# Moving linear attention ahead of the last pair of softmax heads, and the output projection's first weight rows ahead of the third pair, in a two-layer decoder trunk

## The chip, the cores and the metric

The kernel runs on one core of one Trainium2 chip. The metric is the device time of one execution in microseconds (us). Five engines work side by side on a core, each through its own list of instructions: TensorE (PE in the profile) multiplies and transposes, VectorE (DVE) and ScalarE (ACT) do the elementwise work, GpSimd (POOL) sets masks, and SyncE (SP) issues the large transfers. An engine that needs another one's result waits on a semaphore.

## The reference

Two layers, each a half-step feed-forward block (ffn1), a mixer, and another half-step feed-forward block (ffn2). The change is in the mixer, on 256 rows of 1024 numbers:

```python
h = _modulate(_rmsnorm(x, mix_norm[l]), sh2, sc2)
proj = h @ mix_w_in[l]
a_q, a_k, a_v, b_u, c_q, c_k, c_v, c_r, c_g = jnp.split(proj, splits, axis=-1)
...
o_a = _merge_heads(_moba_attention(qa, ka, va))      # 8 heads of 64: causal softmax over the 256 rows
o_b = _conformer_conv(b_u, ...)                      # 256 channels: 31 taps, layer norm, swish
...
o_c = _gla(...)                                      # linear attention, 4 heads, chunks of 64 rows
o_c = _merge_heads(_rmsnorm(o_c, gla_out_norm[l])) * jax.nn.silu(c_r)
mixed = jnp.concatenate([o_a, o_b, o_c], axis=-1) @ mix_w_out[l]
x = x + gt2[:, None, :] * mixed
```

## The kernel before

All of it is float32 in and out. A weight piece comes from memory as `raw` (1 MB by one transfer of SP's queue, five buffers), is cast to a rounded high part `wh` on ACT (L342), and the rest `wl` is taken on DVE (L345); this pair of steps is `split`, and `wh` and `wl` have six buffers each, two for a piece. A product with split operands is three matmuls (L374 to L376 or L735 to L737 in the projections, L990 to L992 in the output projection). Rows that need no split are used as they came (`whole`, L987).

The mixer function `mix(l, done)` runs once per layer. Its program order around the change: projections for the softmax heads; then `attend(0)` to `attend(3)`, one call for each pair of heads, and between them the projections of linear attention. One call of `attend` is a chain over three engines: scores on PE (L865), masked maximum on DVE (L873, L877), exponentials on ACT (L396, four of them), reciprocal on DVE (L883), scaling on ACT (L885), transposes on PE (L888), copies on ACT (L889), products with the values on PE (L895), and the result's split on ACT and DVE (L707, L708). Linear attention is: keys and queries scaled by decays (L905, L906, L911), transposed keys (L922), the scores inside a chunk (L928) and their mask (L933), values to `cv` (L917), chunk states (L945, L951, L956), output (L960, L963), then its norm: square on ACT (L968), group mean on PE (L690), four steps on ACT (L396, L699, L396, L701) and DVE (L702, L703, L971, L973). The convolution is 62 small DVE instructions (L769), handed out in portions by `taps`, and then a norm of its own with the same lines L690 to L703.

The output projection adds four pieces of two 128-row blocks each into four accumulators `acc`. A block's number k says whose output it multiplies: 0 to 3 the softmax pairs, 4 and 5 the convolution, 6 and 7 linear attention.

```python
ORDER = (0, 2, 6, 4)
...
        for n, k0 in enumerate(ORDER):
            ...
            w = (whole if k0 >= 4 else split)(wo[:, k0:k0 + 2, :], [2, D])
```

A scheduler places the instructions of each engine at build time, by the program's order and its own estimate of when an operand is ready. What it printed is fixed: on the chip each engine takes its instructions in that order. Products into one accumulator stay in the program's order.

Of the kernel before, what the change touches and what calls it, by code (L numbers as in the profile page):

```python
# [8 lines left out]
F32 = mybir.dt.float32  # L9
# [4 lines left out]
ALU = mybir.AluOpType  # L14
# [3 lines left out]
P = 128  # L18
T = 256
D = 1024  # L20
KD = 8
# [21 lines left out]
DELAY = 2, 1  # L43
RAW, WHL = 5, 6
TAPS = (4, 2, 4, 4, 4, 4)
ORDER = (0, 2, 6, 4)

PLAN = {None: (0, 0, 0, 1), (0, 0): (22, 0, 0, 30), (0, 1): (0, 0, 0, 1), (0, 2): (19, 0, 5, 28), (1, 0): (15, 0, 5, 28),
        (1, 1): (0, 0, 0, 1), (1, 2): (4, 0, 2, 14)}
# [10 lines left out]
def trunk_kernel(ctx: ExitStack, tc: tile.TileContext, x, c, positions, ada_w, ada_b, ffn1_norm, ffn1_w_in,  # L60
# [4 lines left out]
    ACT, DVE, PE, POOL = nc.scalar, nc.vector, nc.tensor, nc.gpsimd  # L65
# [8 lines left out]
    def nm(s):  # L74
        uid[0] += 1
        return f"{s}_{uid[0]}"
# [5 lines left out]
    def unit(shape, dt=F32, s="u"):  # L82
        return u2.tile(shape, dt, tag="u2k", name=nm(s))
# [4 lines left out]
    def wide():  # L88
        return bank("mm")
# [621 lines left out]
    def mix(l, done):  # L711
        begin(l, 1)
        wi = mix_w_in[l].rearrange("(k p) f -> p k f", p=P)
        mixT = {}
        c2 = lambda ap: ap.rearrange("p a b -> p (a b)")

# [4 lines left out]
        def product_t(c0):  # L721
            return product(split(wi[:, :, c0:c0 + 256], [KD, 256]))

        def proj_n(c0, n):

            nk = 2048 // n
            pp = [wide(), wide()]
            for k0 in range(0, KD, nk):
                wh, wl = split(wi[:, k0:k0 + nk, c0:c0 + n], [nk, n])
                for k in range(nk):  # L730
                    for t in range(2):
                        a = high(k0 + k)[:, P * t:P * t + P]
                        b = low(k0 + k)[:, P * t:P * t + P]
                        first, last = k0 + k == 0, k0 + k == KD - 1
                        PE.matmul(pp[t][:, 0:n], a, wh(k, 0, n), start=first, stop=False)  # L735
                        PE.matmul(pp[t][:, 0:n], b, wh(k, 0, n), start=False, stop=False)  # L736
                        PE.matmul(pp[t][:, 0:n], a, wl(k, 0, n), start=False, stop=last)  # L737
            return pp
# [46 lines left out]
        def taps(n):  # L785
            for _ in range(n):
                next(conv, None)
# [20 lines left out]
        u, e = unit([P, 2, T], F32, "gu"), unit([P, 2, T], F32, "ge")  # L808
# [6 lines left out]
        G, eG = unit([P, 8, 64], F32, "G"), unit([P, 8, 64], F32, "eG")  # L815
# [13 lines left out]
        for w in range(2):  # L829
# [8 lines left out]
            for h in range(2):  # L838
# [3 lines left out]
                a, b = hd3(tmp[0]), hd3(tmp[1])  # L842
# [61 lines left out]
        pk = product_t(2304)  # L904
        DVE.tensor_mul(ke, pk, ke)  # L905
        DVE.tensor_mul(kt, pk, kt)  # L906
        attend(1)
        taps(TAPS[3])
        qt = unit([P, 2, T], F32, "qt")
        pq = product_t(2048)  # L910
        DVE.scalar_tensor_tensor(qt, pq, 0.125, c2(eG).rearrange("p (a b) -> p a b", a=2), op0=ALU.mult, op1=ALU.mult)  # L911
        attend(2)
        taps(TAPS[4])
        cv = unit([P, 2, 256], F32, "cv")
        pv = proj_n(2560, 256)
        for h in range(2):
            ACT.copy(cv[:, h, :], pv[h][:, 0:256])  # L917

        tk = bank()
        for t in range(2):  # L920
# [1 line left out]
                PE.transpose(tk[:, P * (2 * t + h):P * (2 * t + h) + P], ke[:, t, P * h:P * h + P], ident)  # L922
        ken = u.rearrange("p a (b c) -> p (a b) c", c=P)
        ACT.copy(ken, tk.rearrange("p (a b) -> p a b", a=4))

        acaus = [unit([P, 4, P], F32, "acaus") for _ in range(2)]
        pA = [bank(), bank()]
# [3 lines left out]
        for s in range(2):  # L931
            POOL.memset(acaus[s], 0.0)
            DVE.copy_predicated(acaus[s], gmask.bitcast(U32).unsqueeze(1).broadcast_to([P, 4, P]),  # L933
                                pA[s].rearrange("p (a b) -> p a b", a=4))
        attend(3)
        taps(TAPS[5])

        pS = [bank(), bank()]
        products = []
        for t in range(2):  # L940
            for n in (1, 0, 2):
                par, h = n % 2, n // 2
# [4 lines left out]
                                              cv[64 * par:64 * par + 64, h, 128 * t + 64 * s:128 * t + 64 * s + 64],  # L947
                                              start=True, stop=True))
        row(products)
        S = unit([P, 3, 2, 64], F32, "S")  # L950
        DVE.tensor_copy(S[:, 0], pS[0][:, 0:128].rearrange("p (a b) -> p a b", a=2))  # L951
        for n in (1, 2):
            par, h = n % 2, n // 2
            for t in range(2):
                o = 128 * h + 64 * t
                DVE.scalar_tensor_tensor(S[:, n, t, :], S[:, n - 1, t, :], eG[:, 4 * t + n, 63:64],  # L956
                                         pS[par][:, o:o + 64], op0=ALU.mult, op1=ALU.add)
# [14 lines left out]
        for t in range(2):  # L972
            DVE.scalar_tensor_tensor(oc[:, t, :], oc[:, t, :], cols[l][:, R_GN:R_GN + 1], cr[:, t, :], op0=ALU.mult,  # L973
                                     op1=ALU.mult)
            mixT[6 + t] = oc[:, t, :]
        taps(CK + 1)

        wo = mix_w_out[l].rearrange("(k p) n -> p k n", p=P)  # L980
        acc = [wide() for _ in range(4)]
        tile_of = lambda d: acc[d // 2][:, T * (d % 2):T * (d % 2) + T]

# [9 lines left out]

        for n, k0 in enumerate(ORDER):
            if n == 3:
                ada(AT_END[l, 1])
                done.last()
            w = (whole if k0 >= 4 else split)(wo[:, k0:k0 + 2, :], [2, D])
            if n < 3:
                for i in range(2):  # L1000
                    for d in range(KD):
                        add(d, k0 + i, i, w, n + i == 0, False)
            else:
                for d2 in range(0, KD, 2):
                    for i in range(2):
                        for d in (d2, d2 + 1):
                            add(d, k0 + i, i, w, False, i == 1)
                    for d in (d2, d2 + 1):
                        residual(tile_of(d), l, 1, d)
                        done(d)  # L1010
# [223 lines left out]
```

## Time and profile before

| what | value |
|---|---|
| median of three runs | 1053.15 us (1052.93 to 1054.54) |
| the profiled execution | 1054.32 us, of which its span 1052.6 us |
| TensorE, share of the span busy | 99% |
| VectorE, ScalarE | 81%, 57% |
| TensorE's mean granted clock | 0.996 of full speed |

The span goes from the first to the last instruction. A matmul's record overlaps the next one's, so a gap shows as idle time only when the engine really ran dry. The profile puts the idle time in brackets behind the instruction that ended it, with what released it.

### The profile page before, as it was taken

To read this page: it belongs to the slowest core of one execution; us is meant where nothing else is said; L and a number is where in the kernel's file an instruction comes from. 1 tells how busy PE (TensorE), PEld (TensorE's weight loads), DVE (VectorE), ACT (ScalarE), POOL (GpSimd) and SP (SyncE) were. 2 spreads that over 40 slices of the span, in tenths; PEclk is the share of its full clock that TensorE was granted. 3 is DMA by queue.
4 is the path that set the end of the run, shared out by engine and by line. 5 is a ranking of instruction groups with operands and counts; after the bars stand their busy time and mean duration, and the time that the engine had idled before them with its cause. 6 is when DMAs were issued, how large, how long until landed. Compare 5 with 4: busy or idle time off the path is not lost.

```text
span 1052.6 us, 17525 instructions
## 1 busy us (share of the span) xinstructions
PE 1037.0 (99%) x6892; PEld 913.1 (87%) x6892; DVE 848.8 (81%) x1408; ACT 599.2 (57%) x1061; POOL 23.0 (2%) x60
## 2 busy tenths in 40 slices
PE   8999999999999999999999999999999999999998
PEld 7899998888888988888889888888879889888887
DVE  3699878879996899998669998866899779866552
ACT  4565454458667665564457555554767666555441
POOL 6000000001000000000000000000000000000000
PEclk9999999999999999999999999999999999999999
DMA  9999989885344679999766999867343445865430
GB/s 315 369 331 349 363 294 329 303 285 170 125 143 144 229 236 322 359 326 316 235 206 220 332 328 309 287 205 239 122 158 121 160 162 190 287 202 181 157 124 21
DMA packets 177603, 251.42 MB, mean 239 GB/s; under 512 B 7514, under 2 KB 156470, under 8 KB 170352
## 3 DMA queue, kind: packets, MB, share of 16 engines
q1 hardware_dynamic: 176480, 249.97, 70.6%
q8 instruction: 54, 0.88, 0.4%
q0 software_dynamic: 1024, 0.32, 0.2%
q14 instruction: 29, 0.24, 0.1%
q10 hardware_dynamic: 16, 0.00, 0.0%
HBM read 249.23 MB, written 1.05 MB: 238 GB/s over the span
## 4 chain that ended last, share of the span: by engine, by line
PE 90%; ACT 3%; DVE 3%; DMA 2%; POOL 1%; issue 0%; POOLq 0%; DVEq 0%; ACTq 0%
PE mm L380 36%; PE mm L381 18%; PE mm L374 7%; PE mm L376 7%; PE mm L375 7%; PE mm L987 3%; PE mm L737 2%; PE mm L735 2%; PE mm L736 2%; ACT wh L342 1%; PE tp L234 1%; DMA adaraw<-in_ada_w_dram 1%; DMA pos<-in_positions_dram 1%; DVE wl L345 1%; PE tp L262 1%; DVE ab L769 1%
## 5 line engine op out<-in xcount | busy, mean ns | idle before, releaser
L345 DVE TENSOR_TENSOR wl<-raw,wh 128x1024 fp32r<-128x1024 f32 (+1 forms) x344 | 384.2, 1128 | 113.8 <-ACT wh L342 107.6
L342 ACT CAST wh<-raw 128x1024 fp32r<-128x1024 f32 (+1 forms) x344 | 332.5, 974 | 235.5 <-PE mm L380 106.2
L380 PE MATMUL mm<-hT,wh 128*128 128x512 f32 x912 | 322.7, 397 | 0.0
L381 PE MATMUL mm<-hT,wl 128*128 128x256 f32 x912 | 256.3, 282 | 0.0
L380 PE MATMUL mm<-g,wh 128*128 128x512 f32 x704 | 249.3, 398 | 0.0
L380 PEld LDWEIGHTS mm<-hT,wh 128*128 128x128 f32 x912 | 172.4, 189 | 43.0 <-DVE g L708 1.7
L381 PE MATMUL mm<-g,wl 128*128 128x256 f32 x704 | 197.6, 281 | 0.0
L374 PE MATMUL mm<-hT,wh 128*128 128x256 f32 (+1 forms) x656 | 188.1, 287 | 2.1 <-ACT wh L342 2.0
L375 PE MATMUL mm<-hT,wh 128*128 128x256 f32 (+1 forms) x656 | 186.9, 285 | 0.0
L376 PE MATMUL mm<-hT,wl 128*128 128x256 f32 (+1 forms) x656 | 186.5, 284 | 0.3 <-DVE wl L345 0.2
L381 PEld LDWEIGHTS mm<-hT,wl 128*128 128x128 f32 x912 | 171.7, 188 | 0.2
L380 PEld LDWEIGHTS mm<-g,wh 128*128 128x128 f32 x704 | 132.2, 188 | 35.0 <-ACT wh L342 2.5
L381 PEld LDWEIGHTS mm<-g,wl 128*128 128x128 f32 x704 | 133.0, 189 | 0.0
L374 PEld LDWEIGHTS mm<-hT,wh 128*128 128x128 f32 x656 | 124.9, 190 | 5.2 <-ACT wh L342 2.6
L376 PEld LDWEIGHTS mm<-hT,wl 128*128 128x128 f32 x656 | 124.8, 190 | 0.9 <-DVE wl L345 0.8
L375 PEld LDWEIGHTS mm<-hT,wh 128*128 128x128 f32 x656 | 124.5, 190 | 1.0 <-DVE hT L461 0.2
L243 DVE SCALAR_TENSOR_TENSOR adaacc<-adaraw,cact,adaacc 128x2048 f32<-128x2048 f32 (+1 forms) x59 | 123.5, 2093 | 2.1 <-DMA adaraw<-in_ada_w_dram 2.1
L553 ACT COPY ab<-mm 128x256 f32<-128x256 f32 x114 | 41.7, 370 | 53.5 <-PE mm L381 53.4
L559 DVE SCALAR_TENSOR_TENSOR xT<-mm,gate,xT 128x256 f32<-128x256 f32 x80 | 34.6, 478 | 22.7 <-PE mm L381 15.3
L554 DVE TENSOR_TENSOR ab<-ab,mm 128x256 f32<-128x256 f32 x114 | 46.3, 416 | 6.2 <-ACT ab L553 6.0
L769 DVE SCALAR_TENSOR_TENSOR ab<-hpad,cw,ab 128x256 f32<-128x256 f32 x120 | 51.0, 476 | 0.0
L737 PE MATMUL mm<-wl,hT 128*128 128x512 f32 (+1 forms) x128 | 47.6, 372 | 0.0
(231 smaller groups left out, 1062.5 us busy)
## 6 DMA issues: line engine op xcount, KB each, us to landing
raw<-in_ffn_w_in_dram SPq DMA_DIRECT2D x85, 1024.0 KB, 6.4
adaraw<-in_ada_w_dram SPq DMA_DIRECT2D x72, 1024.0 KB, 7.0
raw<-in_ffn_w_out_dram SPq DMA_DIRECT2D x32, 1024.0 KB, 6.1
raw<-in_mix_w_in_dram SPq DMA_DIRECT2D x24, 1024.0 KB, 5.6
raw<-in_ffn_w_out_dram SPq DMA_DIRECT2D x16, 768.0 KB, 5.7
raw<-in_mix_w_out_dram SPq DMA_DIRECT2D x8, 1024.0 KB, 5.0
held<-in_ffn_w_in_dram SPq DMA_DIRECT2D x12, 256.0 KB, 10.5
xn<-in_x_dram SPq DMA_DIRECT2D x2, 512.0 KB, 4.3
```

The lines of the kernel that those rows point to most:

```text
L243: DVE.scalar_tensor_tensor(part, w, cact[:, k, 0:1], part, op0=ALU.mult, op1=ALU.add)
L342: ins = ACT.copy(hs[-1][:, b:c], raw(a + b, a + c)).ins
L345: DVE.tensor_sub(ls[-1][:, b:c], raw(a + b, a + c), f32(hs[-1][:, b:c]))
L374: PE.matmul(o, wh, high, start=first, stop=False)
L375: PE.matmul(o, wh, low, start=False, stop=False)
L376: PE.matmul(o, wl, high, start=False, stop=last)
L380: PE.matmul(halves(o), wh, pair, start=first, stop=False)
L381: PE.matmul(o[:, 0:T], wl, pair[:, 0, :], start=False, stop=last)
L553: ACT.copy(t[:, s, :], o[s][:, T:2 * T])
L554: DVE.tensor_add(t[:, s, :], t[:, s, :], o[s][:, 0:T])
L737: PE.matmul(pp[t][:, 0:n], a, wl(k, 0, n), start=False, stop=last)
L769: DVE.scalar_tensor_tensor(y[:, t, :], hpad[:, t, k:k + T], w, y[:, t, :], op0=ALU.mult, op1=ALU.add)
```

## The change

Linear attention up to its norm stands ahead of `attend(3)`: the key transposes ahead of `attend(1)`, the chunk scores and their mask ahead of `attend(2)`, states, output and norm between `attend(2)` and `attend(3)`. The split of the value projection's weights (`wv`) and that of the output projection's first piece (`w0`, rows of the softmax pairs 0 and 1) stand ahead of `attend(2)`. `ORDER` takes linear attention's rows second. The states `S` are kept in a tile that is free by then.

```diff
-ORDER = (0, 2, 6, 4)
+ORDER = (0, 6, 2, 4)
...
-        attend(1)
-        taps(TAPS[3])
-        qt = unit([P, 2, T], F32, "qt")
-        pq = product_t(2048)
-        DVE.scalar_tensor_tensor(qt, pq, 0.125, c2(eG).rearrange("p (a b) -> p a b", a=2), op0=ALU.mult, op1=ALU.mult)
-        attend(2)
-        taps(TAPS[4])
-        cv = unit([P, 2, 256], F32, "cv")
-        pv = proj_n(2560, 256)
-        for h in range(2):
-            ACT.copy(cv[:, h, :], pv[h][:, 0:256])
 
         tk = bank()
...
         ACT.copy(ken, tk.rearrange("p (a b) -> p a b", a=4))
+        attend(1)
+        taps(TAPS[3])
+        qt = unit([P, 2, T], F32, "qt")
+        pq = product_t(2048)
+        DVE.scalar_tensor_tensor(qt, pq, 0.125, c2(eG).rearrange("p (a b) -> p a b", a=2), op0=ALU.mult, op1=ALU.mult)
...
-        attend(3)
-        taps(TAPS[5])
+        wv = split(wi[:, :, 2560:2816], [KD, 256])
+
+        w0 = split(wo[:, ORDER[0]:ORDER[0] + 2, :], [2, D])
+        attend(2)
+        taps(TAPS[4])
+        cv = unit([P, 2, 256], F32, "cv")
+        pv = proj_n(2560, 256, wv)
+        for h in range(2):
+            ACT.copy(cv[:, h, :], pv[h][:, 0:256])
...
-        S = unit([P, 3, 2, 64], F32, "S")
+
+        S = c2(e)[:, 0:384].rearrange("p (n a b) -> p n a b", n=3, a=2)
...
             mixT[6 + t] = oc[:, t, :]
+        attend(3)
+        taps(TAPS[5])
         taps(CK + 1)
...
-            w = (whole if k0 >= 4 else split)(wo[:, k0:k0 + 2, :], [2, D])
+            w = (whole if k0 >= 4 else split)(wo[:, k0:k0 + 2, :], [2, D]) if n else w0
```

From `attend` on, the changed kernel's line numbers are one higher (L888 is L889 there), the output projection's four higher (L990 is L994).

The first place is PE's list in the second layer, from the last pair's scores (`tp<-qkT`) to the first transposes of its softmax (`tp<-ident,tmp`). Before:

```order
L865 MATMUL tp_8822<-qkT_8140,qkT_8138 128x128
L865 MATMUL tp_8821<-qkT_8140,qkT_8138 128x128
L992 MATMUL mm_8976<-mix_8487,wl_8983 128x256
L990 MATMUL mm_8976<-mix_8487,wh_8982 128x256
...
L990 MATMUL mm_8978<-mix_8606,wh_8986 128x256
L888 MATMUL tp_8841<-ident_70,tmp_8133 128x128 [waits Activation_49]
L991 MATMUL mm_8978<-mix_8606,wh_8986 128x256
L992 MATMUL mm_8978<-mix_8606,wl_8987 128x256
L888 MATMUL tp_8841<-ident_70,tmp_8133 128x128 [waits Activation_49]
```

And in the changed kernel:

```order
L690 MATMUL tp_8872<-ge_8118,grpb_86 128x256
L866 MATMUL tp_8888<-qkT_8138,qkT_8136 128x128 [waits PE_49]
...
L994 MATMUL mm_8987<-mix_8611,wh_8715 128x256
L995 MATMUL mm_8987<-mix_8611,wh_8715 128x256
L996 MATMUL mm_8987<-mix_8611,wl_8716 128x256
L889 MATMUL tp_8907<-ident_70,tmp_8132 128x128 [waits PE_49,Activation_49]
L889 MATMUL tp_8907<-ident_70,tmp_8132 128x128 [waits Activation_49]
L889 MATMUL tp_8907<-ident_70,tmp_8132 128x128
L991 MATMUL mm_8984<-G_8125,raw_9036 128x256 [waits DMAHW1_49,DVE_49]
L991 MATMUL mm_8984<-G_8125,raw_9036 128x256
L889 MATMUL tp_8924<-ident_70,tmp_8133 128x128 [waits PE_49,Activation_49]
```

Before, 36 products of the output projection stand between the scores and the first transpose (34 in the first layer). Now it is the last three of the first piece (eight in the first layer); the products of the linear-attention rows (`mm<-G,raw`) stand behind the transposes, and the 48 products of the pairs 2 and 3 behind those.

The second place is ACT's list in the second layer at the same point: `tmp` and `nb` belong to the last pair's softmax, `rstd` to linear attention's norm, `wh` to ffn2's weights. Before:

```order
L396 ACTIVATE tmp_8133,rsum_8834<-tmp_8133,nb_8832,rq_1313_8143 128x128 [waits DVE_49]
L396 ACTIVATE tmp_8133,rsum_8834<-tmp_8133,nb_8832,rq_1313_8143 128x256
L342 CAST wh_9197<-raw_9195 128x512 [waits DMAHW5_49,PE_49]
L342 CAST wh_9197<-raw_9195 128x512
L885 ACTIVATE tmp_8133<-tmp_8133,rin_8837 128x128 [waits DVE_49]
```

And in the changed kernel:

```order
L396 ACTIVATE rstd_8875<-tp_8872,epsc_80 128x512 [waits PE_49]
L699 ACTIVATE rstd_8876<-tp_8872,hepsc_82 128x512
L396 ACTIVATE rstd_8875<-rstd_8875 128x512 [waits Activation_49]
L342 CAST wh_9201<-raw_9193 128x512 [waits PE_49]
L701 ACTIVATE rstd_8877<-rstd_8875 128x512 [waits Activation_49]
L396 ACTIVATE tmp_8132,rsum_8900<-tmp_8132,nb_8898,rq_1312_8142 128x128 [waits DVE_49]
L396 ACTIVATE tmp_8132,rsum_8900<-tmp_8132,nb_8898,rq_1312_8142 128x256
L342 CAST wh_9201<-raw_9193 128x512
L886 ACTIVATE tmp_8132<-tmp_8132,rin_8903 128x128 [waits DVE_49]
```

The four steps of the norm now stand ahead of the last pair's exponentials. In the first layer they do too, there without a cast among them and with all four exponentials ahead of the first scaling.

The third place is DVE's list in the second layer between the second pair's second reciprocal and the third pair's first maximum (`mx`). Before:

```order
L883 RECIPROCAL rin_8592<-rsum_8589 128x2 [waits Activation_49]
L769 SCALAR_TENSOR_TENSOR ab_7993<-hpad_105,cw_21_118,ab_7993 128x256 [waits DVE_49] x11
L911 SCALAR_TENSOR_TENSOR qt_8617<-mm_8628,eG_8127 128x512 [waits PE_49]
L708 TENSOR_TENSOR mix_8606<-tp_8601,mix_8606 128x256 [waits Activation_49]
L873 ISA tmp_8133,mx_8686<-tp_8678,amask_90 128x128 [waits PE_49]
```

And in the changed kernel:

```order
L884 RECIPROCAL rin_8597<-rsum_8594 128x2 [waits Activation_49]
L770 SCALAR_TENSOR_TENSOR ab_7992<-hpad_105,cw_21_118,ab_7992 128x256 [waits DVE_49] x10
L919 SCALAR_TENSOR_TENSOR qt_8622<-mm_8633,eG_8126 128x512 [waits PE_49]
L708 TENSOR_TENSOR mix_8611<-tp_8606,mix_8611 128x256 [waits Activation_49]
L770 SCALAR_TENSOR_TENSOR ab_7992<-hpad_105,cw_21_118,ab_7992 128x256 [waits DVE_49] x4
L928 COPY_PREDICATED acaus_8684<-gmask_98,tp_8686 128x512 [waits PE_49,Pool_49]
L928 COPY_PREDICATED acaus_8683<-gmask_98,tp_8685 128x512 [waits PE_49]
L770 SCALAR_TENSOR_TENSOR ab_7992<-hpad_105,cw_21_118,ab_7992 128x256 [waits DVE_49]
L874 ISA tmp_8132,mx_8727<-tp_8719,amask_90 128x128 [waits PE_49]
```

Five taps and the two masks have come in ahead of the third pair's maximum, for one tap fewer earlier.

## Rows read from the trace of the kernel before

**Rows 1.** The page: the chain that ended last, and one group (busy us, mean ns).

```profile
PE 90%; ACT 3%; DVE 3%; DMA 2%; POOL 1%; issue 0%; POOLq 0%; DVEq 0%; ACTq 0%
...
L342 ACT CAST wh<-raw 128x1024 fp32r<-128x1024 f32 (+1 forms) x344 | 332.5, 974 | 235.5 <-PE mm L380 106.2
```

**Rows 2.** Windows: length, busy PE, PEld, DVE, ACT, POOL; then granted clock.

```profile
728.00:861.50 133.50, 130.23 (x906) 112.44 (x906) 113.28 (x261) 89.33 (x182) 0.99 (x2) 0.99 0.45 150
312.00:324.00 12.00, 10.90 (x103) 10.13 (x103) 11.07 (x32) 9.65 (x25) 0.00 (x0) 1.00 0.89 285
818.78:822.20 3.42, 3.42 (x20) 2.40 (x22) 3.42 (x4) 1.94 (x5) 0.00 (x0) 0.50 0.01 4
```

**Rows 3.** Timeline of PE, second layer, third pair: start, us, what, [idle before].

```profile
815.81 0.28 PE L991 MATMUL mm<-mix,wh 128*128 128x256 f32 x1
816.40 1.53 PE L888 MATMUL tp<-ident,tmp 128*128 128x128 f32 x6 [0.31 <-ACT tmp L885]
818.74 1.55 PE L895 MATMUL tp<-tmp,va 128*64 128x256 f32 x8 [0.81 <-ACT tmp L889]
...
823.45 0.38 PE L992 MATMUL mm<-mix,wl 128*128 128x256 f32 x1
```

**Rows 4.** The same work in the first layer.

```profile
310.65 0.87 PE L895 MATMUL tp<-tmp,va 128*64 128x256 f32 x8
311.46 0.66 PE L922 MATMUL tp<-ident,ge 128*128 128x128 f32 x4
...
313.04 0.94 PE L865 MATMUL tp<-qkT,qkT 64*128 64x128 f32 x12
313.91 0.38 PE L992 MATMUL mm<-mix,wl 128*128 128x256 f32 x1
```

**Rows 5.** Timeline of PE, first layer, last pair's first transpose.

```profile
317.84 0.28 PE L990 MATMUL mm<-mix,wh 128*128 128x256 f32 x1
317.96 0.28 PE L991 MATMUL mm<-mix,wh 128*128 128x256 f32 x1
319.34 0.33 PE L888 MATMUL tp<-ident,tmp 128*128 128x128 f32 x1 [1.10 <-ACT tmp L885]
319.43 0.36 PE L992 MATMUL mm<-mix,wl 128*128 128x256 f32 x1
```

**Rows 6.** Timeline of PE, both layers: the first product of linear attention's rows.

```profile
334.49 1.78 PE L987 MATMUL mm<-G,raw 128*128 128x256 f32 x7 [0.26 <-DVE G L973]
...
843.87 1.35 PE L987 MATMUL mm<-G,raw 128*128 128x256 f32 x5 [1.61 <-DVE G L973]
```

**Rows 7.** Timeline of all engines, second layer: the third pair's softmax.

```profile
811.52 0.94 PE L865 MATMUL tp<-qkT,qkT 64*128 64x128 f32 x12
...
812.87 0.28 DVE L873 CUSTOM_DVE_ANT_0 tmp<-tp,amask 128x128 f32<-128x128 f32 x1
...
813.82 0.49 ACT L396 ACTIVATE tmp<-tmp,nb,rq 128x128 f32<-128x128 f32 x1 [1.40 <-DVE nb L877]
...
815.96 1.48 ACT L885 ACTIVATE tmp<-tmp,rin 128x128 f32<-128x128 f32 x4
```

**Rows 8.** Timeline of ACT, first layer: linear attention's norm, and what follows.

```profile
329.28 0.70 ACT L396 ACTIVATE rstd<-tp,epsc 128x512 f32<-128x512 f32 x1
...
331.65 0.62 ACT L773 ACTIVATE ab<-ab 128x512 f32<-128x512 f32 x1
```

**Rows 9.** Timeline of ACT, second layer: after the third pair's value products.

```profile
820.33 0.37 ACT L707 CAST mix<-tp 128x256 fp32r<-128x256 f32 x1 [1.12 <-PE tp L895]
820.60 0.65 ACT L917 COPY cv<-mm 128x256 f32<-128x256 f32 x2
```

**Rows 10.** Timeline of DVE, second layer, ahead of the third pair's maximum.

```profile
807.59 4.42 DVE L769 SCALAR_TENSOR_TENSOR ab<-hpad,cw,ab 128x256 f32<-128x256 f32 x11
811.93 0.68 DVE L911 SCALAR_TENSOR_TENSOR qt<-mm,eG 128x512 f32<-128x512 f32 x1
...
822.97 1.35 DVE L933 COPY_PREDICATED acaus<-gmask,tp 128x512 f32<-128x512 uint32 x2 [0.56 <-PE tp L928]
```

More of the change, by code (lines that the diff above doesn't have):

```diff
@@ L713, in mix @@
         wi = mix_w_in[l].rearrange("(k p) f -> p k f", p=P)
+        wo = mix_w_out[l].rearrange("(k p) n -> p k n", p=P)
         mixT = {}
@@ L722, in product_t, with proj_n @@
             return product(split(wi[:, :, c0:c0 + 256], [KD, 256]))
-        def proj_n(c0, n):
+        def proj_n(c0, n, w=None):
             nk = 2048 // n
@@ L728, in proj_n @@
             for k0 in range(0, KD, nk):
-                wh, wl = split(wi[:, k0:k0 + nk, c0:c0 + n], [nk, n])
+                wh, wl = w or split(wi[:, k0:k0 + nk, c0:c0 + n], [nk, n])
                 for k in range(nk):
@@ L975, in mix @@
             mixT[6 + t] = oc[:, t, :]
+        attend(3)
+        taps(TAPS[5])
         taps(CK + 1)
-        wo = mix_w_out[l].rearrange("(k p) n -> p k n", p=P)
         acc = [wide() for _ in range(4)]
```

## The prediction

> **What bounds the kernel now.** I read the chain that ended last first: 90% of the span is TensorE's [rows 1]. The kernel gets shorter only where TensorE waits or its clock is low. So I went through TensorE's timeline in both mixers for instructions with idle time in brackets, and read the windows for the clock: the whole second mixer shows 0.99, with one stretch of 3.42 us at 0.50 in it [rows 2], which is 1.2 of 2.4 GHz. The reader is to see five places. In the second layer the six transposes of the third pair wait for ScalarE, and the value products behind them again [rows 3]: from 816.09 (end of the last product) to 818.74 it is 2.65 us for six transposes, which at 0.16 us each (four of the same size take 0.66 [rows 4]) are 1.0 us of work, so 1.65 us of waiting. Right behind that the clock stands at 0.50: value products, key transposes, chunk scores and the last pair's scores take 4.71 us [rows 3], and in the first layer at full clock 3.26 [rows 4], so 1.45 us more. In the first layer the last pair's first transpose waits 1.10 us [rows 5], and the clock stays at 1.00 there [rows 2]. And in both layers the first product of linear attention's rows waits for the norm, 0.26 and 1.61 us [rows 6].
>
> **What the change takes away.** All five, if it does what it does to the order: the norm is finished long before its products in the place where they waited, the third pair's transposes have 33 products ahead of them in place of 29, and the key transposes and chunk scores stand elsewhere. That is 1.10 + 0.26 in the first layer, 1.65 + 1.45 + 1.61 in the second: 6.1 us. More isn't to be had at these places, and less if one of the waits stays; I take all of it.
>
> **What it puts in their place.** The work on every engine is the same in sum: no matmul, cast or transfer is added, and the states take one tile less. What counts is what stands between an instruction and its operand.
>
> First, the last pair's transposes. Between its scores and the first transpose there were 36 and 34 products; now there are three in the second layer and eight in the first. The 24 products of pair 2 can't come forward, since they add to accumulators that linear attention's rows must add to first, and those wait for the norm; the 24 of the last pair need this softmax itself. So TensorE waits for a whole softmax with nothing to do. The third pair shows its length: scores from 811.52, done 0.87 later (313.04 to 313.91 [rows 4]) at 812.39, first transpose at 816.40 [rows 3, 7], so 4.0 us. Against it stand products of 0.12 us each [rows 5]: three give 0.36, eight give 0.96. That is the lower bound, 3.65 and 3.05, 6.7 us together. But ScalarE now has the norm's four steps first, 2.37 us from 329.28 to 331.65 [rows 8]; it can begin them when the group mean is done, when TensorE begins the scores. In the first layer then come four exponentials, 2.14 us from 813.82 to 815.96, and 0.44 from the first scaling to the transpose [rows 3, 7]: 4.95, less scores 0.87 and eight products 0.96, so 3.1 us. In the second layer two exponentials (1.07) and two half casts, about 0.5 each (a whole one takes 0.97 [rows 1]): 4.9, less 0.87 and 0.36, so 3.65. I take 6.8 us; VectorE's steps of the norm, which stand between those of the softmax, may add 0.5 in each layer, so the upper bound is 7.8.
>
> Second, `cv`. The chunk states need the two copies to `cv`, which ScalarE makes behind the split of the third pair's result; from the end of the value products to the end of the copies it is 0.92 us, 820.33 to 821.25 [rows 9]. This was hidden, since transposes, chunk scores and the last pair's scores came next on TensorE. Now one product of 0.12 stands there in the second layer (0.8 us of waiting), and one matmul of another kind in the first, for which I take 0.4: 1.2 us. Nothing else can stand in, so 0.8 is the least.
>
> Third, the third pair's own transposes. VectorE now reaches its maximum later: ten taps at 0.40 (4.42 for eleven [rows 10]), queries and result split 0.94 (811.93 to 812.87 [rows 7, 10]), four taps 1.6, two masks 1.35 [rows 10], a tap 0.4, in all 8.3 us. They began at 807.59 [rows 10]; a split of 1.1 us ahead of them has gone elsewhere and a tap of 0.4 has come, so they begin at 806.9 and the maximum starts at 815.2, the first transpose 3.53 us later (812.87 to 816.40 [rows 3, 7]), at 818.7. TensorE had begun the third pair's scores at 811.52 [rows 7]; before that point it now does four transposes more (0.6) and eight products less (0.96), so 811.15, then nine products (1.1), chunk scores and scores (1.85, from 313.91 less 311.46 less 0.6 [rows 4]) and 33 products (3.95), which ends at 818.05. It waits 0.65 us, and some 0.4 more for the second head. Both sides are sums over many rows, and an error of 1 us is easy: the bounds are 0 and 2 us in each layer, and I take 1.2 each, 2.4 us.
>
> Fourth, small ones with one answer: in the second layer linear attention's products, among the last pair's transposes, may wait for the norm's steps on VectorE (0 to 1 us, I take 0.5), and ffn2's opening may find its operands later, because a transfer for the modulation now waits for a buffer that those products hold and VectorE's use of it stands ahead of the first residual (0 to 1, I take 0.3). The earlier split of `w0` costs nothing: VectorE does the same two subtractions, and TensorE has products of the projections to do meanwhile; without that cover it would cost their 2.3 us (1.13 each).
>
> Fifth, the clock. In the second layer some 1.65 us of waiting in 2.65 came before the fall, and the fall cost 1.45; 1.10 us in the first layer brought none [rows 2, 3, 5]. The new waits are 3.1 and 3.65 us, longer than the one that brought the fall, so I count two falls. Part of each slow stretch will lie in further waits, where it costs nothing: 1.2 us each, 2.4 together, with 0 and 2.9 as bounds. The Trainium skill says, in TensorE: Matmul & The Clock Gate, section HAM oscillation — how this bites in real kernels, that a wait for operands between groups of products re-throttles the engine, so that the next group starts cold, and it prices the loss at half of the throttled time. By that price, an estimate, two stretches of 3.42 us would cost 3.4 us in place of 2.4 and the sum would be 1.0 us higher; the row's own 1.45 is less than half of 3.42, because not all that ran in it ran on the array all the time, and I keep to it.
>
> **Sum.** New: 6.8 + 1.2 + 2.4 + 0.8 + 2.4 = 13.6 us; gone: 6.1; so 7.5 us longer. The profiled execution took 1054.32 us; its sum would be 1061.8. The median of the runs is 1.17 us lower than it, 1053.15, so I predict 1060.7 for the median. A measurement of this kernel can tell about 0.2%, 2.1 us, from no change.
>
> **Rivals.** *The cover holds (faster).* TensorE finds work behind each waiting transpose, or the softmax is done when it gets there; only `cv` is left: 1.2 less 6.1, 4.9 us shorter, 1048.3. It speaks for it that 24 products, those of pair 2, have their operands before the last pair's softmax ends. Against it: in the first layer TensorE sat 1.10 us at a transpose, and the product behind it started 0.09 us after it [rows 5], although its operands came from pairs long done: it doesn't pass a waiting instruction. It decides for faster only if all new waits but `cv` and the clock's share stay under 2.8 us together, against 6.7 that the third pair's own softmax gives for the first alone. The Trainium skill says the same in TensorE: Matmul & The Clock Gate, Part 2: What happens when you issue a matmul: weight loads may be pulled ahead, the matmuls themselves stay in program order. The trace agrees, by the 1.10 us. Chance 0.05.
>
> *Only the last pair and `cv` (no change).* The third pair's transposes find their operands ready and the clock doesn't fall: 6.8 + 1.2 less 6.1, 1.9 us longer, 1055.1. For it: my count for the third pair is near zero within its error; the clock held through 1.10 us. Against: the waits are three times that. Chance 0.12.
>
> *Everything at its upper end (slower still).* 7.8 + 1.2 + 4 + 2 + 2.9 less 6.1, 11.8 us longer, 1065. For it: DVE and ACT take norm and softmax in turns, so each late step makes the other late. Chance 0.13.
>
> **How the numbers follow.** The forecast has 0.70, and with its small terms off by one or two it spans 1057 to 1063. The range from 1055.5 to 1065 leaves out the faster case, most of the no-change case and what lies beyond the upper end. Slower by over 0.2% is the forecast and the upper case, 0.83; within 0.2% is the third, 0.12; faster 0.05.
>
> **What would show it.** In the profile after: the last pair's transposes with 3 to 4 us of idle time in front of them in each layer, released by the scaling on ScalarE, and the norm's four steps ahead of the exponentials; the chunk states with about half a us or more, released by the copies to `cv`; two stretches at clock 0.5 behind the long waits; no idle time in front of linear attention's products at their old size in the second layer, and the stretch at 818.78 at full clock. I am wrong if TensorE's idle time at the last pair's transposes is under 2 us in a layer, or if products of pair 2 run there.

## The result: 10.5 us slower

The changed kernel takes 1064.57 us (median of 5 runs, 1063.33 to 1065.29) where the kernel before, run beside it, takes 1054.03; the ratio is 1.0099, 95% interval 1.0088 to 1.011. The profiled span went from 1052.6 to 1063.6 us.

The changed kernel's page, the chain that ended last; in [rows 1] TensorE has 90% of it:

```profile
PE 87%; DVE 5%; ACT 4%; DMA 3%; issue 1%; SPq 0%; ACTq 0%
```

To see where the time went I cut out each mixer, from the first pair's first score to the next stage's first product. Windows of the kernel before (start and end, length, busy PE, PEld, DVE, ACT, POOL, granted clock):

```profile
282.66:348.22 65.56, 64.20 (x525) 55.58 (x525) 54.51 (x152) 45.58 (x106) 0.00 (x0) 1.00 0.49 161
791.91:857.60 65.69, 62.81 (x506) 55.71 (x505) 53.34 (x141) 44.75 (x104) 0.00 (x0) 0.97 0.43 144
```

The same windows of the changed kernel, and its stretches of low clock:

```profile
282.91:354.58 71.67, 68.54 (x525) 57.37 (x525) 54.77 (x151) 45.20 (x104) 0.00 (x0) 0.98 0.44 146
798.31:868.11 69.80, 64.52 (x505) 56.25 (x505) 53.32 (x139) 43.90 (x100) 0.00 (x0) 0.95 0.42 138
329.90:333.32 3.42, 3.42 (x10) 2.60 (x10) 1.58 (x4) 2.07 (x5) 0.00 (x0) 0.50 0.00 0
841.90:848.73 6.83, 6.10 (x17) 4.15 (x19) 1.11 (x4) 2.17 (x6) 0.00 (x0) 0.50 0.49 154
```

The first mixer is 6.11 us longer and the second 4.11, together 10.2 of the 11.0 us. Length less busy PE is idle time: 1.36 became 3.13 in the first mixer, 2.88 became 5.28 in the second, so 4.2 us. The other 6 us lie in a *busy* TensorE with the same instructions, 4.34 us of them in the first mixer. So idle time alone explains less than half.

The rows that answer to [rows 3, 5, 6], TensorE's timeline of the changed kernel in both mixers:

```profile
324.21 0.94 PE L866 MATMUL tp<-qkT,qkT 64*128 64x128 f32 x12
...
329.42 0.33 PE L889 MATMUL tp<-ident,tmp 128*128 128x128 f32 x1 [3.12 <-ACT tmp L886]
329.70 1.06 PE L991 MATMUL mm<-G,raw 128*128 128x256 f32 x2
...
825.03 0.33 PE L889 MATMUL tp<-ident,tmp 128*128 128x128 f32 x1 [0.48 <-ACT tmp L886]
...
829.13 0.84 PE L947 MATMUL tp<-cv,gu 64*64 64x64 f32 x24 [0.43 <-ACT cv L938]
...
836.01 0.94 PE L866 MATMUL tp<-qkT,qkT 64*128 64x128 f32 x12
...
840.86 0.83 PE L889 MATMUL tp<-ident,tmp 128*128 128x128 f32 x3 [3.36 <-ACT tmp L886]
842.63 2.07 PE L991 MATMUL mm<-G,raw 128*128 128x256 f32 x4 [0.94 <-DVE G L976]
```

The last pair's transposes wait 3.12 and 3.36 us, with a fall of the clock behind each. ScalarE's timeline in the second mixer shows what they wait for:

```profile
836.12 0.69 ACT L396 ACTIVATE rstd<-tp,epsc 128x512 f32<-128x512 f32 x1 [0.76 <-PE tp L690]
...
838.30 0.64 ACT L701 ACTIVATE rstd<-rstd 128x512 f32<-128x512 f32 x1
838.83 0.48 ACT L396 ACTIVATE tmp<-tmp,nb,rq 128x128 f32<-128x128 f32 x1
...
839.89 0.60 ACT L342 CAST wh<-raw 128x512 fp32r<-128x512 f32 x1
840.40 0.80 ACT L886 ACTIVATE tmp<-tmp,rin 128x128 f32<-128x128 f32 x2
...
843.08 0.80 ACT L886 ACTIVATE tmp<-tmp,rin 128x128 f32<-128x128 f32 x2 [0.28 <-DVE rin L884]
```

The norm's steps, with a half cast among them, fill 836.12 to 838.94; only then come the softmax's exponentials.

### The profile page after: what moved, and what is told of

Its sections match the earlier page's. It is cut to its first block, busy times and chain, and to the rows that moved or that the text cites. A ratio compares the mean times of both kernels' runs of the same rounds, so it can differ in the third digit from the quotient of the medians.

```text
span 1063.6 us, 17530 instructions
## 1 busy us (share of the span) xinstructions
PE 1043.7 (98%) x6892; PEld 915.6 (86%) x6892; DVE 849.1 (80%) x1408; ACT 599.2 (56%) x1061; POOL 22.9 (2%) x60
## 4 chain that ended last, share of the span: by engine, by line
PE 87%; DVE 5%; ACT 4%; DMA 3%; issue 1%; SPq 0%; ACTq 0%
PE mm L380 36%; PE mm L381 18%; PE mm L374 7%; PE mm L376 7%; PE mm L375 6%; PE mm L991 2%; DMA adaraw<-in_ada_w_dram 2%; DVE wl L345 2%; DMA held<-in_ffn_w_in_dram 1%; PE mm L738 1%; DVE ab L770 1%; PE mm L737 1%; PE mm L736 1%; ACT wh L342 1%; PE tp L262 1%; PE tp L234 1%
## 5 line engine op out<-in xcount | busy, mean ns | idle before, releaser
L737 PE MATMUL mm<-wh,hT 128*128 128x512 f32 (+1 forms) x128 | 47.6, 372 | 0.0
L736 PE MATMUL mm<-wh,hT 128*128 128x512 f32 (+1 forms) x128 | 47.5, 371 | 0.0
```

## The experiments

Lengths are those of the two mixers in the profiled execution, cut as above; the last column is idle PE in them (length less busy PE). Each ratio is against the kernel before as it was run beside that version (medians 1054.03 to 1054.29).

| kernel | median, us | ratio to before | mixer 1 | mixer 2 | idle 1, 2 |
|---|---|---|---|---|---|
| before | 1054.03 | | 65.56 | 65.69 | 1.36, 2.88 |
| changed | 1064.57 | 1.0099 (1.0088 to 1.011) | 71.67 | 69.80 | 3.13, 5.28 |
| e1_order_back | 1062.85 | 1.0083 (1.0069 to 1.0097) | 71.22 | 68.47 | 2.08, 4.41 |
| e2_early_split | 1059.58 | 1.0052 (1.0039 to 1.0065) | 67.51 | 68.44 | 2.62, 5.04 |
| e3_filled_wait | 1058.96 | 1.0047 (1.0034 to 1.0059) | 69.99 | 65.76 | 1.21, 2.53 |
| e4_early_gla | 1061.71 | 1.0065 (1.0051 to 1.0079) | 68.22 | 69.93 | 1.55, 4.70 |
| e5_norm_behind | 1057.87 | 1.0037 (1.0024 to 1.005) | 67.94 | 66.95 | 1.16, 3.24 |
| e6_e1_norm_behind | 1056.20 | 1.0019 (1.001 to 1.0028) | 68.82 | 64.09 | 0.93, 1.83 |
| e7_order_alone | 1068.56 | 1.0143 (1.0129 to 1.0157) | 70.96 | 74.79 | 6.38, 8.86 |
| e8_filled_before | 1054.01 | 1.0 (0.9992 to 1.0009) | 65.47 | 65.82 | 1.27, 3.45 |
| e9_second_layer_only | 1052.71 | 0.9986 (0.9977 to 0.9995) | 65.39 | 64.11 | 1.17, 1.84 |
| e10_scores_cut | 1056.15 | 1.002 (1.0011 to 1.0029) | 67.57 | 65.81 | 0.59, 1.97 |
| e11_scores_whole | 1054.89 | 1.001 (1.0001 to 1.0019) | 66.09 | 64.94 | 0.41, 2.41 |

**e1, the old order of rows in the changed kernel.**

```diff
-ORDER = (0, 6, 2, 4)
+ORDER = (0, 2, 6, 4)
```

> The changed kernel with one line put back: the output projection adds the rows of pairs 0 and 1 first, then those of pairs 2 and 3's first half as before, linear attention's third (0, 2, 6, 4). Linear attention stays ahead of the last pair and the early splits stay. TensorE's order now has 30 products (first layer) and 25 (second) between the last pair's scores and its first transpose, where the changed kernel has 8 and 3. Theory 'no cover': the cost of the change is that nothing can run during the last pair's softmax, and the clock falls behind that wait. From the scores' end to the first transpose the changed kernel takes 4.35 us and 3.98 us; 30 and 25 products of 0.12 us are 3.7 and 3.1, so 0.6 and 0.9 us of waiting stay of 3.12 and 3.36, the 0.94 us in front of linear attention's first product goes, and with them both falls of the clock, some 4 us: about 1054.7 us, between 1053 and 1057. Rival 'early norm': the norm's steps ahead of the softmax on ScalarE and VectorE make everything behind them late, whatever TensorE has to do: within 3 us of the changed kernel, 1061.5 or more.

1062.85: the theory "no cover" falls in that form (cover: products that TensorE can run while a chain on other engines isn't done). The rival's 1061.5 or more is met; e5 and e6 below take up the norm's place. TensorE's timeline of e1, second mixer, and the second head's transposes in the kernel before:

```profile
835.34 0.94 PE L866 MATMUL tp<-qkT,qkT 64*128 64x128 f32 x12
...
840.19 0.84 PE L889 MATMUL tp<-ident,tmp 128*128 128x128 f32 x3 [0.73 <-ACT tmp L886]
843.43 1.09 PE L889 MATMUL tp<-ident,tmp 128*128 128x128 f32 x3 [2.40 <-ACT tmp L886]
845.08 1.55 PE L896 MATMUL tp<-tmp,va 128*64 128x256 f32 x8 [0.57 <-ACT tmp L890]
```

```profile
831.09 0.33 PE L888 MATMUL tp<-ident,tmp 128*128 128x128 f32 x1
```

The first head's wait is what I expected (0.73 for 0.9). I had not counted the second head, which comes 3.24 us behind the first, and the clock falls within its wait (0.50 from 842.31 on, for 6.83 us). From scores to the second head's transposes it is 8.1 us. In the kernel before it is no shorter: 8.4, from 822.69 to 831.09. But there 60 products of 0.12 us lie within it. They are the 72 products of pairs 0 to 2 less four that had run before and eight that run later; in e1 47 of the 72 had run before the last pair's scores, in the stages where the change put linear attention.

**e2, the early splits alone, in the kernel before.**

```diff
+        wv = split(wi[:, :, 2560:2816], [KD, 256])
+        w0 = split(wo[:, ORDER[0]:ORDER[0] + 2, :], [2, D])
         attend(2)
...
-        pv = proj_n(2560, 256)
+        pv = proj_n(2560, 256, wv)
```

> The kernel before with the early splits alone: the split of the value weights and of the output projection's first rows ahead of the third pair's call, linear attention and the order of rows as before. TensorE then has 33 products ahead of the third pair's first transposes in place of 29, and more behind them. Theory 'the early split costs nothing and takes the third pair's wait away': the second layer's 1.65 us and the 1.45 us of low clock behind it go: about 1051 us, between 1049.5 and 1052.5. Rival 'the early split brings the loss': its casts and subtractions stand in the way of the softmax's steps, so the transposes wait as long as before or longer: 1054 or more, and if it were the whole cause of the loss, 1064.

1059.58: the rival's side, but not by its mechanism. TensorE's timeline of e2, second mixer: the third pair's first transpose, the last pair's, the norm's matmuls and the first product of linear attention's rows:

```profile
818.54 0.27 PE L889 MATMUL tp<-ident,tmp 128*128 128x128 f32 x1
...
828.77 0.33 PE L889 MATMUL tp<-ident,tmp 128*128 128x128 f32 x1 [0.36 <-ACT tmp L886]
...
839.61 1.09 PE L690 MATMUL tp<-ge,grpb 128*128 128x256 f32 x4
...
847.32 1.22 PE L989 MATMUL mm<-G,raw 128*128 128x256 f32 x2 [3.10 <-DVE G L976]
```

The third pair's wait is gone, as the first theory said, and the clock stays up there; the last pair waits 0.36 us. But 21 products of pairs 0 and 1 now run ahead of the last pair in the second mixer, where 4 did, so only 6 are left between the norm's matmuls and linear attention's products, which wait 3.10 us, with a fall of the clock at 846.90. In the first mixer 14 are left and the wait is 2.62 us, there without a fall. The cover was spent early and is missing at the end.

**e3, the wait of the changed kernel filled.**

```diff
+                for _ in range(fill if s == 0 else 0):
+                    PE.transpose(pT[:, 0:P], ident, ident)
...
-        attend(3)
+        attend(3, 18)
```

> The changed kernel with 18 transposes of the identity (18 x some 0.16 us = 2.9 us) put on TensorE between the last pair's scores and its first transposes in each mixer, written to a place that the true transpose writes over. They use the time of the wait and add nothing to the result. Theory 'the clock pays a part': the waits of 3.12 and 3.36 us become work of the same length, so the time of the waits stays, but the clock doesn't fall behind them: by the rows of the changed kernel the products in the slow stretches take some 1.4 us (first layer) and 2.5 us (second) more than at full clock, so about 1061 us, between 1059.5 and 1062.5. Rival 'the wait alone': the low clock costs nothing, because what runs in it would wait for linear attention's norm anyway: within 0.8 us of the changed kernel, 1063.8 to 1065.4.

1058.96, 5.6 us faster than the changed kernel although 36 instructions were added. Windows of e3, and its timeline:

```profile
282.00:351.99 69.99, 68.78 (x543) 58.17 (x543) 54.77 (x151) 45.20 (x104) 0.00 (x0) 1.00 0.45 150
795.84:861.60 65.76, 63.23 (x524) 56.48 (x523) 53.47 (x139) 43.70 (x101) 0.00 (x0) 1.00 0.43 142
```

```profile
324.17 2.19 PE L889 MATMUL tp<-ident 128*128 128x128 f32 x18
326.11 0.36 PE L997 MATMUL mm<-mix,wh 128*128 128x256 f32 x1
...
328.51 0.33 PE L891 MATMUL tp<-ident,tmp 128*128 128x128 f32 x1 [1.21 <-ACT tmp L886]
...
838.55 0.33 PE L891 MATMUL tp<-ident,tmp 128*128 128x128 f32 x1 [1.61 <-ACT tmp L886]
```

The clock reads 1.00 in both. The filling takes 1.94 us (324.17 to 326.11) in each mixer; busy PE without it is 66.84 and 61.29 us, against 68.54 and 64.52 in the changed kernel. So the low clock cost 1.70 and 3.23 us in the changed kernel's profiled execution, and in the second mixer idle time fell by 0.8 besides: there the scheduler has also put some of linear attention's products elsewhere among the transposes, and their wait of 0.94 us is gone. In the first mixer the order is otherwise the same. The theory holds in its direction, with a larger price than it named: 1058.96 lies below its 1059.5.

**e4, linear attention early, alone** (no early splits, old order of rows).

```diff
-        w0 = split(wo[:, ORDER[0]:ORDER[0] + 2, :], [2, D])
...
-            w = (whole if k0 >= 4 else split)(wo[:, k0:k0 + 2, :], [2, D]) if n else w0
+            w = (whole if k0 >= 4 else split)(wo[:, k0:k0 + 2, :], [2, D])
```

> Linear attention up to its norm ahead of the last pair, alone: the order of the rows as before (0, 2, 6, 4) and no early split. TensorE has 34 and 29 products between the last pair's scores and its first transpose, but only some 16 and 18 between the third pair's scores and its transposes, where the changed kernel has 34 and 33. Theory 'no cover': the wait goes to the third pair: by the changed kernel's rows its transposes are ready 4.7 us behind the scores' end in the second layer, 18 products are 2.2, so 2.4 us of waiting and a fall of the clock there, up to 2 us in the first layer, against e1's about 1054.7: about 1058 us, between 1055.5 and 1061. Rival 'early norm': the loss belongs to the place of linear attention itself and comes back whole: 1062 or more.

1061.71, between the two. The third pair's wait in the second mixer is 2.30 us, as expected, with its fall of the clock; but the last pair waits again as well, 1.62 and 0.57 us, and brings another fall.

**e5 and e6, the norm behind the last pair.** The edit is the same on e4 and on e1:

```diff
+        attend(3)
+        taps(TAPS[5])
         oc, osq = G.rearrange("p (a c) b -> p a (c b)", a=2), e
...
-        attend(3)
-        taps(TAPS[5])
         taps(CK + 1)
```

> e4_early_gla (linear attention early, rows in the old order, no early split) with the last pair's call put between linear attention's output and its norm, so that ScalarE and VectorE come to the last pair's softmax first and to the norm's steps behind it. Theory 'two chains at once': norm and softmax together take the 7 to 9 us from the scores to the second head's transposes, and 24 to 34 products of 0.12 us don't last that long. With the norm behind, the last pair's waits (1.62 and 0.57 us in the second layer, 0.82 and 0.59 in the first) and the fall of the clock there go, some 5 us, and up to 1 us comes back in front of linear attention's products: about 1057 us against 1061.7, between 1055 and 1059. The third pair's wait of 2.3 us stays. Rival 'the cover is spent': products used up before the last pair are missing whatever stands first, so the wait goes over to the norm whole: 1060 or more.

> The same step from e1_order_back (which has the early splits): the last pair's call between linear attention's output and its norm. Theory 'two chains at once': e1's waits at the last pair (0.50, 0.87 and 0.57 us in the first layer, 0.73, 2.40 and 0.57 in the second) and its falls of the clock (some 1.4 and 3.2 us) go, 10 us, and 1 to 3 us come back in front of linear attention's products, which have 24 products ahead of them where e2_early_split had 14 and 6 and waited 2.62 and 3.10: about 1056 us, between 1053.5 and 1058.5, and by the third pair's wait better than e5_norm_behind. Rival 'the cover is spent': 1060 or more, the wait standing in front of linear attention's products with a fall of the clock behind it.

1057.87 and 1056.20, 3.8 and 6.7 us faster than e4 and e1, where 4.7 and 7 were expected, so the rival falls. ScalarE's timeline of e6, second mixer:

```profile
833.48 0.49 ACT L396 ACTIVATE tmp<-tmp,nb,rq 128x128 f32<-128x128 f32 x1
...
835.61 1.48 ACT L886 ACTIVATE tmp<-tmp,rin 128x128 f32<-128x128 f32 x4
...
840.40 0.69 ACT L396 ACTIVATE rstd<-tp,epsc 128x512 f32<-128x512 f32 x1 [0.29 <-PE tp L690]
```

Softmax first, then the norm. TensorE's timeline of e6:

```profile
836.05 0.33 PE L889 MATMUL tp<-ident,tmp 128*128 128x128 f32 x1
...
838.43 0.87 PE L896 MATMUL tp<-tmp,va 128*64 128x256 f32 x8 [0.84 <-ACT tmp L890]
...
845.60 1.78 PE L991 MATMUL mm<-G,raw 128*128 128x256 f32 x7 [0.22 <-DVE G L978]
```

Both heads' transposes find their operands, linear attention's products wait 0.22 us where they waited 1.61 [rows 6], and the clock doesn't fall in either mixer. The second mixer is 1.6 us *shorter* than in the kernel before; the first stays 3.3 us longer, with less idle time than before: its TensorE is busy for 67.89 us in place of 64.20, at full clock.

Two things moved with this edit. From the end of the last pair's scores to the second head's transposes it is 5.2 us in e6 (831.65 to 836.80) where e1 took 7.2 (836.21 to 843.43): the chain is shorter with the norm behind it. And the scores come earlier in TensorE's order: 26 of the 72 products have run before them, not 47, so 45 lie in that stretch, not 25. The times fit "two chains at once"; how much of the gain each of the two brings was not separated.

**e7, the order of rows alone, in the kernel before.**

```diff
-ORDER = (0, 2, 6, 4)
+ORDER = (0, 6, 2, 4)
```

> The kernel before with the changed order of rows alone (0, 6, 2, 4): linear attention's rows come ahead of pair 2's, everything else in its old place. Theory 'no cover': in the kernel before 24 and 17 products stand between the norm's first matmul and linear attention's products, which wait 0.26 and 1.61 us; without them the waits are about 3.3 and 3.7 us, so 5.1 us more, and each lets the clock fall, 1.5 us in each layer: about 1062 us, between 1059 and 1064.5. Rival 'the order is a detail': the 24 products of pair 2 run a little later and nothing else changes: 1054 to 1055.5.

1068.56, the slowest of all. The theory is right in sign, but 6.5 us too low and outside its range, and the loss is not where it put it. Linear attention's products wait 1.65 and 2.09 us, less than the 3.3 and 3.7 expected; here in the second mixer:

```profile
850.73 8.60 PE L987 MATMUL mm<-G,raw 128*128 128x256 f32 x32 [2.09 <-DVE G L973]
```

Besides them both heads of the last pair, the value products and both norms' matmuls wait, and the second mixer's clock falls twice (10.2 us at 0.50).

**e8, the third pair's wait of the kernel before filled** (second mixer), by the loop of e3.

```diff
-        attend(2)
+        attend(2, 10 if l == 1 else 0)
```

> The kernel before with ten transposes of the identity (10 x 0.11 us) ahead of the third pair's transposes in the second mixer alone, where it waits 0.31 and 0.81 us and the clock falls; they are written over and add nothing to the result. Theory 'the clock pays a part': the wait is 1.65 us with what drains and restarts, the transposes stand in for most of it, the clock stays up and the 1.45 us behind it go: about 1052.7 us, between 1051.8 and 1053.4. Rival 'filling costs what it takes': the same as before or up to 1.1 us more, 1054 to 1055.3.

1054.01, no change: the rival's number, though not its reason. TensorE's timeline of e8:

```profile
811.83 0.94 PE L865 MATMUL tp<-qkT,qkT 64*128 64x128 f32 x12
...
821.62 1.12 PE L865 MATMUL tp<-qkT,qkT 64*128 64x128 f32 x12
...
828.23 0.33 PE L890 MATMUL tp<-ident,tmp 128*128 128x128 f32 x1 [0.99 <-ACT tmp L885]
```

The clock stays at 1.00 and the last pair's scores come 9.79 us behind the third pair's, where they came 11.17 behind (811.52 [rows 7] to 822.69): 1.4 us gained. Then the last pair's transposes wait 0.99 us, where they had no wait, and start as late as before: 35.97 us behind the mixer's start, against 35.96. The chain there doesn't follow TensorE: VectorE comes to the maximum 0.5 us earlier, and ScalarE's cast ahead of the first scaling then waits 0.57 us for a transfer. So the 1.45 us of low clock in the kernel before, which I had booked as a gain, was paid out of a wait for the softmax behind it.

The other executions of the kernel before say the same. Their mean granted clock goes from 0.996 to 1.0, so the fall isn't in all of them, and the 19 at 0.999 or 1.0 take 1054.1 us in the mean, the nine at 0.996 1054.3.

**e9, the second mixer of e6, the first of the kernel before.**

```diff
+        early = l == 1
...
+        if early:
+            ken = key_transposes()
         attend(1)
...
-        pO = output()
+        if early:
+            pO = output()
+        else:
+            ken = key_transposes()
+            acaus = chunk_scores()
         attend(3)
         taps(TAPS[5])
+        if not early:
+            pO = output()
```

> The first mixer in the order of the kernel before, the second in that of e6_e1_norm_behind (linear attention up to its output ahead of the last pair, the early splits, the last pair's call between output and norm, old order of rows). From the last pair's first stage to the next stage e6's second mixer took 64.1 us where the kernel before took 65.7, and its first mixer 68.8 where before took 65.6. Theory 'the layers add up': 1.6 us faster than the kernel before, about 1052.7 us, between 1051.8 and 1053.6. Rival 'only moved': what the second mixer gives comes back in the stage behind it, or hung on the first mixer's order: 1054 or more.

1052.71, ratio 0.9986: the layers add up, and this version is faster than both kernels, by 1.5 us (1054.19 beside it) and 11.9 us.

**e10 and e11, what a cut in a row of scores costs.** In the changed kernel's first mixer two rows of scores are cut, each by four products, and the modulation's sums stand elsewhere. TensorE's timeline of the changed kernel, and the sums in the kernel before:

```profile
293.08 0.49 PE L866 MATMUL tp<-qkT,qkT 64*128 64x128 f32 x2
293.50 0.38 PE L375 MATMUL mm<-hT,wh 128*128 128x256 f32 x1
...
294.17 0.93 PE L866 MATMUL tp<-qkT,qkT 64*128 64x128 f32 x10
...
314.68 1.44 PE L262 MATMUL tp<-adaacc,ones 128*32 128x512 f32 x5
316.05 0.87 PE L896 MATMUL tp<-tmp,va 128*64 128x256 f32 x8
316.85 1.05 PE L262 MATMUL tp<-adaacc,ones 128*32 128x512 f32 x2
```

```profile
309.67 1.06 PE L262 MATMUL tp<-adaacc,ones 128*32 128x512 f32 x6
```

The group of the modulation's sums in the first mixer (busy us, mean ns), in the kernel before and then in the changed one:

```profile
L262 PE MATMUL tp<-adaacc,ones 128*32 128x512 f32 x8 | 2.1, 605 | 0.0
```

```profile
L262 PE MATMUL tp<-adaacc,ones 128*32 128x512 f32 x8 | 2.9, 598 | 0.0
```

e10 cuts all eight rows of the kernel before with one transpose each; e11 has the same transposes ahead of the rows. In both mixers TensorE's order differs in nothing else. The edit of e10:

```diff
+                    if len(products) == 1:
+                        products.append(PE.transpose(ss[0][:, 0:P], ident, ident))
```

> The kernel before with one transpose of the identity (0.11 us, written over later, nothing in the result) between the first and the other five score matmuls of each pair, eight times in all: it cuts each row of 64-row matmuls as the changed kernel's and e1's orders cut three of them in the first mixer. Theory 'changes of kind cost': a row of scores takes 0.87 us uncut, and in the changed kernel's rows a cut one takes some 0.6 us more beside the four products in the cut, so 8 x 0.5 = 4 us more than e11, which has the same eight transposes ahead of the rows; less where TensorE waits for the softmax anyway: 2 to 4.5 us over e11. Rival 'the products only swap places': less than 0.8 us between the two.

> The control to e10_scores_cut: the same eight transposes of the identity ahead of each pair's row of scores, which stays whole; everything else in the same order as there. By both theories 8 x 0.11 = 0.9 us over the kernel before at most: 1054 to 1055.5.

1056.15 against 1054.89, and spans of 1055.6 against 1053.2 us. Timelines of e10 and e11, first mixer's last pair:

```profile
315.05 0.38 PE L865 MATMUL tp<-qkT,qkT 64*128 64x128 f32 x2
315.37 0.33 PE L868 MATMUL tp<-ident 128*128 128x128 f32 x1
315.63 0.93 PE L865 MATMUL tp<-qkT,qkT 64*128 64x128 f32 x10
```

```profile
314.16 0.33 PE L861 MATMUL tp<-ident 128*128 128x128 f32 x1
314.42 0.94 PE L865 MATMUL tp<-qkT,qkT 64*128 64x128 f32 x12
```

Busy PE in the two mixers is 130.82 against 128.21 us: 0.33 us for each of the eight cuts. The size was overrated (0.5). Of the 2.6 us, 2.4 reach the end by the two profiled spans and 1.3 by the medians, which is less than the 2 expected. The medians alone don't rule the rival's 0.8 out, since the two ratios' intervals overlap; the busy time does.

## Why the prediction was right, and where its sum was not

Direction and range were right, and the likeliest case happened: the last pair's transposes wait for a whole softmax. The size was 3 us short. By the number alone the rival "everything at its upper end" (1065) came nearer, but not by its terms: it put 4 us on the third pair, where 0.48 was measured, and 2.9 on the clock, where 4.93 was. By the prediction's steps:

- **The last pair, 3.1 and 3.65 us:** measured 3.12 and 3.36. The norm's four steps do stand ahead of the exponentials, and products of linear attention among the transposes wait 0.94 us for the norm (0.5 taken). ffn2's first product waits in neither layer. Of the 0.8 us left over outside the mixers 0.25 lies ahead of the first mixer, 0.04 between the two and 0.5 behind the second; it was not followed further.
- **`cv`, 0.4 and 0.8 us:** 0 and 0.43. In the first mixer two sums of the modulation ran in the place of the wait.
- **The third pair, 1.2 and 1.2 us:** no wait in the first mixer, 0.48 us in the second. Here the prediction took a value above its own count of 0.65, and the count was nearer.
- **"The earlier split of `w0` costs nothing":** failed. No wait in e2's mixers is for its casts, but the split lets products run early that are the cover of later waits; with the split of the value weights, and nothing else, it costs 5.5 us (e2). What it costs hangs on the rest of the order: beside early linear attention it is 1.1 us (e1 against e4), and with the norm behind the last pair the version with the splits is 1.7 us the faster (e6 against e5). The changed kernel without the splits was not run.
- **The clock, 1.2 us for each fall:** mis-sized, with 1.70 and 3.23 measured (e3). The second stretch was 6.83 us long, not 3.42, and the discount for further waits inside it was wrong: in the changed kernel what runs there is on the path. The reason given for a price under half, that not all in the stretch ran on the array all the time, isn't borne out by the row, which has 3.42 us of busy PE in 3.42 [rows 2]. And a long wait doesn't always bring a fall: in e2's first mixer 2.62 us brought none. The rule of the Trainium skill that the prediction weighed and set aside (TensorE: Matmul & The Clock Gate, HAM oscillation — how this bites in real kernels: half of the throttled time) gives, as an estimate, 1.7 and 3.4 for stretches of 3.42 and 6.83. The trace agrees with it within 0.2 us here, but not for the kernel before, whose stretch cost nothing (e8).
- **The 1.45 us of low clock taken away:** the fall is gone, but e8 shows that it cost the kernel before nothing.
- **What was missing altogether:** order on a busy TensorE. Busy PE of the first mixer without filling is 66.84 us in e3 against 64.20 before, with no low clock in either: 2.64 us for the same 525 instructions. Two cuts of scores are some 0.7 of it by e10; the modulation's sums are 0.8 (2.1 to 2.9 us above): up to three of these matmuls of 32 columns started together before, at most two do now. The remaining 1.1 us was not taken apart, and its cause stays open. In the second mixer, where no row is cut, order costs nothing (61.29 us in e3 against 62.81 less 1.45).

Idle time +4.2, low clock 4.93 less 1.45, order +2.6: 10.2 us for the two mixers. Forecast were, in nearly the same terms, 6.6 (11.2 new, 4.6 gone), 0.95 (2.4 less 1.45) and 0; only its 1.65 us for the third pair is more than the 0.31 and 0.81 that the profile shows as idle there. So idle time was overrated by as much as each of the other two was underrated, and the sum came out nearer than its parts: that was luck.

The rival "the cover holds" fell as its argument said: no product passes a waiting transpose. But the mechanism was told too narrowly. That pair 2's products stand behind linear attention's is one way to bare the last pair; e1 gives them back and gains 1.7 us, while the same order of rows alone costs 14.3 (e7): the steps of the change don't add up one by one. What e1 to e7 show together is a fixed stock of 72 products of pairs 0 to 2, some 8.6 us, and 24 more behind the last softmax, against two chains that ScalarE and VectorE serve in turn: some 8 us from the last pair's scores to its second head's transposes, some 6.5 from the norm's matmuls to linear attention's products. The change put both chains side by side and had spent more than half of the stock before they began; with the softmax ahead of the norm (e5, e6) the softmax has 44 and 45 products to cover it in the second mixer, and the norm the last 24.

## What to carry to other kernels

Products whose operands are ready early are a stock: before starting them sooner, find the wait that they cover now. Don't let two chains over the same slow engine begin together; give the one that TensorE meets first the engine first. And compare busy time as well as idle time, window by window: here more than half of the loss was a busy TensorE, at a low clock and in another order.

## What was not expected of the hardware

- Eighteen transposes of the identity ahead of a wait kept the granted clock at 1.00 in both mixers, though 1.21 and 1.61 us of the wait remained; they made the kernel 5.6 us faster (e3).
- A row of twelve 64-row score matmuls takes 0.33 us more when one 128-row instruction stands in it, with no idle time shown. The Trainium skill says in TensorEngine Tiling (Array Packing), Key Properties, that a change of the tiling mode drains the engine. The price fits that, by e10 against e11; that it is a drain the trace doesn't show.
- Low clock cost 3.23 us in one order, in a stretch of 6.83, and nothing in another, in a stretch of 3.42 (e3, e8): what it costs depends on whether a slower engine sets the pace behind it.
